# A hybrid decoder trunk on one core: SwiGLU's first products as paired 512-column streams, with modulation steps shifted later

## The chip, the cores and the metric

The kernel runs on one core of a Trainium2 chip. The metric is the device time of one execution in microseconds (us). Engine names follow the profile: PE is TensorE's matrix product, PEld its weight loads, DVE is VectorE, ACT is ScalarE, SP the queue that issues most transfers.

## The reference

Two layers, batch 1, 256 positions, width 1024, all in float32. Each layer is three residual blocks. Each block starts with an RMS norm and a modulation whose shift, scale and gate are parts of `silu(c) @ ada_w[l] + ada_b[l]` (a vector of 9 x 1024).

```python
h = _modulate(_rmsnorm(x, ffn1_norm[l]), sh1, sc1)
x = x + 0.5 * gt1 * _swiglu(h, ffn1_w_in[l], ffn1_w_out[l])   # (silu(a) * b) @ w_out, [a|b] = h @ w_in, 2816 wide
h = _modulate(_rmsnorm(x, mix_norm[l]), sh2, sc2)
...                                   # attention, conv and gated linear attention from one projection
x = x + gt2 * mixed
h = _modulate(_rmsnorm(x, ffn2_norm[l]), sh3, sc3)
x = x + 0.5 * gt3 * _swiglu(h, ffn2_w_in[l], ffn2_w_out[l])
```

## The kernel before

**Float32 as two parts.** Every weight and every operand is split into a high part and a low part of a type that PE multiplies in one pass. A product is high x high + weight high x operand low + weight low x operand high. `mm3` (L347 to L349) issues these as three matmuls of 256 columns, `mm2` (L353, L354) as one of 512 columns, whose moving operand is [high | low] side by side, and one of 256 columns. With `mm2` the two halves of a 512-column result still have to be added.

**A piece.** `split` loads 1 MB of a weight matrix (`raw`, 5 buffers, shared with the modulation's matrices), ACT copies it to the high part `wh` (L327, two tiles of 128x1024), DVE subtracts to get the low part `wl` (L328). `wh` and `wl` have 6 tiles each: three pieces. At the end of each `split` a planner (`PLAN`: steps m, lo, hi for each phase) issues steps of the modulation's product: each takes 1 MB of `ada_w` and one DVE instruction over 128x2048 (L232; the first of a group is L230). A group's sum goes through PE (L251, L263) two and three pieces later. `AT_END` issues further steps on PE near a phase's end.

**An FFN phase**, `ffn(l, i)`, four of them. The operand `hT` holds high and low for each of 8 k blocks, in rows of 258. Its first matrix has 22 pieces (11 for a, 11 for b). The first two are an `opening` that starts before the norm is known; the others go through `product`: 8 k x 2 halves x `mm3` = 48 matmuls into one PSUM bank (`wide`, tag "mm", four banks; a second set of four banks has the tag "tp"). ACT then reads a's bank (Silu, L369), DVE multiplies by b's bank (L592), and `split_out` (L642 on ACT, L643 on DVE) makes the two parts of the result. The second matrix has 12 pieces in four groups and uses `mm2`, with two banks for each group; DVE adds the results to the residual stream `xT` (L516). Phase (0, 0) differs: `open_first` does the first three products before it, so it counts 30 pieces and not 34.

**A mix phase** uses `product` for six matrices and `proj_n` (L670 to L672) for the others. The low-rank gate's product at L738 uses the [high | low] rows of `hT` as one 512-column operand.

The engines run their queues in the order in which the framework's planner wrote them; each queue is strictly in order.

Of the kernel before, what the change touches and what calls it, by code (L numbers as in the profile page):

```python
# [8 lines left out]
F32 = mybir.dt.float32  # L9
# [8 lines left out]
P = 128  # L18
# [33 lines left out]
EARLY = {(0, 1): (6,), (0, 2): (4,), (1, 0): (6,), (1, 1): (6,), (1, 2): (4,)}  # L52
LATE = 1
PART = 1024
FIRST, SECOND, AHEAD = 0, 2, 0
# [4 lines left out]
def trunk_kernel(ctx: ExitStack, tc: tile.TileContext, x, c, positions, ada_w, ada_b, ffn1_norm, ffn1_w_in,  # L60
# [24 lines left out]
    def bank(tag="tp"):  # L85
        return psum.tile([P, 512], F32, tag=tag, name=nm(tag), bufs=4)

    def wide():
        return bank("mm")

    def halves(t):
        return t.rearrange("p (a b) -> p a b", a=2)
# [212 lines left out]
    def split(src, shape, fine=False, held=None):  # L305
# [33 lines left out]
        m, tensor, lo, hi = PLAN[state["phase"]]  # L339
        at = lambda x: m * min(max(x - lo, 0), hi - lo) // (hi - lo)  # L340
        for x in range(at(state["piece"] - 1), at(state["piece"])):
# [9 lines left out]
    def mm2(o, wh, wl, pair, first, last):  # L351

        PE.matmul(o, wh, pair, start=first, stop=False)  # L353
        PE.matmul(o[:, 0:T], wl, pair[:, 0:T], start=False, stop=last)  # L354

# [148 lines left out]
    def product(w):  # L504

        wh, wl = w
        o = halves(wide())
        for k in range(KD):
            for s in range(2):
                cs = P * s, P * s + P  # L510
                mm3(o[:, s, :], wh(k, *cs), wl(k, *cs), high(k), low(k), k + s == 0, k + s == KD)
        return o

    def residual(o, l, i, d):
# [4 lines left out]
    def emit(d):  # L519

        if d % 2 == 0 and d < 6:
            return
        ds = [d] if d >= 6 else [d - 1, d]
        n = P * len(ds)
        t = halves(wide())
        ob = unit([P, 2, T], F32, "ob")
        for h in range(2):
            for i, e in enumerate(ds):
                PE.transpose(t[:, h, P * i:P * i + P], xT[:, e, P * h:P * h + P], ident)
        ACT.copy(ob[:, :, 0:n], t[:, :, 0:n])  # L530
        nc.sync.dma_start(out[0].rearrange("(h p) n -> p h n", p=P)[:, :, P * ds[0]:P * ds[0] + n], ob[:, :, 0:n])


    def ffn(l, i, w_in, w_out, done, first=None):
# [19 lines left out]
        if first is None:  # L554
            piece(1)
            pps = [[wide(), wide()] for _ in range(2)]
            opening(l, i, ws, pps, {HOOKS[l, i][0]: mean_square, HOOKS[l, i][1]: spread})
        else:
            ws += first[:4]
        for ch in range(KF // 2):  # L560
# [4 lines left out]
            if first is not None and ch < 2:  # L565
                if ch == 0:
                    continue
                pb = product(piece(3))
                opened, bias = first[4:]
# [10 lines left out]
            elif ch == 0:  # L580
                (a, ba), (b, bb) = rms(pps[0]), rms(pps[1])
                piece(1, SECOND)
                modulated(l, i)
                for s in range(2):
                    act(a[:, s, :], a[:, s, :], AF.Silu, bias=ba[:, s, :])
                    DVE.scalar_tensor_tensor(a[:, s, :], b[:, s, :], bb[:, s, :], a[:, s, :], op0=ALU.add,
                                             op1=ALU.mult)
            else:
                pa, pb = (product(piece(2 * ch + n, AHEAD)) for n in range(2))
                a = unit([P, 2, T], F32, "ab")  # L590
                act(a, pa, AF.Silu)
                DVE.tensor_mul(a, a, pb)  # L592
            gated(a)
        wo = w_out[l].rearrange("(k p) n -> p k n", p=P)
        late = []
        for grp2 in range(4):
            pp = [wide(), wide()]
            for k0 in range(0, KF, 8):
# [5 lines left out]
                for k, j in order:  # L604
                    g = gT[k0 + k]
                    mm2(pp[j], wh(k, P * j, P * j + P), wl(k, P * j, P * j + P), g, k0 + k == 0, k0 + k == KF - 1)
                while late:
# [38 lines left out]
    def mix(l, done):  # L646
# [12 lines left out]
        def proj_n(c0, n):  # L659

            nk = 2048 // n
            pp = [wide(), wide()]
            for k0 in range(0, KD, nk):
# [18 lines left out]
        ws = [split(wi[:, :, c0:c0 + 256], [KD, 256], fine=True) for c0 in (1792, 1536)]  # L682
        pps = [[wide(), wide()] for _ in range(2)]
        opening(l, 1, ws, pps, hooks={HOOKS[l, 1][0]: mean_square, HOOKS[l, 1][1]: spread})
# [231 lines left out]
        wo = mix_w_out[l].rearrange("(k p) n -> p k n", p=P)  # L916
        acc = [wide() for _ in range(4)]
        tile_of = lambda d: acc[d // 2][:, T * (d % 2):T * (d % 2) + T]
# [72 lines left out]
    def open_first():  # L991


        wi = ffn1_w_in[0].rearrange("(k p) (ab f) -> p k ab f", p=P, ab=2)
        held, ws, outs = [[] for _ in range(3)], [], []

        def load(m):
            ws.append(split(wi[:, :, m % 2, T * (m // 2):T * (m // 2) + T], [KD, T], fine=True, held=held[m]))

        def products(m, k0, k1):  # L1000
            if k0 == 0:
                outs.append(halves(wide()))
            wh, wl = ws[m]
            for k in range(k0, k1):
                for s in range(2):
                    cs = P * s, P * s + P
                    mm3(outs[m][:, s, :], wh(k, *cs), wl(k, *cs), high(k), low(k), k + s == 0, k + s == KD)
# [11 lines left out]
        for j in range(2):  # L1019
            for d2 in range(2):  # L1020
                t = halves(wide())
                for i in range(2):
# [105 lines left out]
```

## Time and profile before

| what | value |
|---|---|
| time, median of 3 runs | 1075.56 us (1074.71 to 1075.88) |
| time of the profiled execution | 1075.7 us |
| its span, first to last instruction | 1073.9 us |
| PE busy | 1053.9 us, 98% of the span |
| DVE busy | 817.0 us, 76% |
| ACT busy | 564.8 us, 53% |
| granted TensorE clock, mean | 0.994 of full speed |

PE's durations overlap: a matmul of 256 columns has a row of about 0.28 us and the next starts 0.12 us after it. What a matmul costs the stream is therefore the distance between starts, or a count over a stretch, and not its row's duration.

### The profile page before, as it was taken

Reading aid. Unit: us, or ns where it says so; the run is one execution under the profiler, and the core shown is the slowest. Engines: PE = TensorE matmul, PEld = TensorE weight load, DVE = VectorE, ACT = ScalarE, POOL = GpSimd, SP = SyncE. Lnnn points to the kernel's source line nnn. Section 1 sums busy time; section 2 is a strip of 40 time slices with the busy share of each in tenths; the row PEclk is TensorE's granted clock in tenths of the full one; section 3 lists DMA queues with packets and bytes.
Section 4 is the critical chain, followed back from the end, with each engine's and each line's share of the span. In section 5 each row is a group of like instructions: output and inputs, shape, how many; then the busy total and the mean of one; then the engine's idle time right before and its main releaser. Section 6 shows DMA issues by size and latency. Waiting matters only on the chain.

```text
span 1073.9 us, 19335 instructions
## 1 busy us (share of the span) xinstructions
PE 1053.9 (98%) x7899; PEld 970.3 (90%) x7899; DVE 817.0 (76%) x1310; ACT 564.8 (53%) x944; POOL 6.5 (1%) x30
## 2 busy tenths in 40 slices
PE   5999999999999999999999999999999999999998
PEld 4799998888888999998889999988878899999987
DVE  3598887979986898888569877766899688755552
ACT  4464454457665854444456444455757485444441
POOL 1000000000000000000000000000000000000000
PEclk8999999999999999999999999999999999999999
DMA  9989999995417389999667898876443446764540
GB/s 305 363 290 356 320 318 311 318 299 163 147 51 234 121 272 372 323 322 325 210 215 246 303 308 283 284 230 229 146 139 109 158 143 208 263 211 160 165 128 20
DMA packets 177593, 251.47 MB, mean 234 GB/s; under 512 B 7372, under 2 KB 156512, under 8 KB 170336
## 3 DMA queue, kind: packets, MB, share of 16 engines
q1 hardware_dynamic: 177272, 250.14, 69.4%
q8 instruction: 62, 1.02, 0.4%
q14 instruction: 27, 0.22, 0.1%
q10 hardware_dynamic: 232, 0.09, 0.0%
HBM read 249.16 MB, written 1.05 MB: 233 GB/s over the span
## 4 chain that ended last, share of the span: by engine, by line
PE 96%; DVE 1%; DMA 1%; ACT 1%; issue 0%; ACTq 0%; DVEq 0%
PE mm L347 18%; PE mm L349 17%; PE mm L348 17%; PE mm L353 15%; PE mm L354 8%; PE mm L671 3%; PE mm L670 2%; PE mm L672 2%; PE mm L923 2%; PE mm L924 1%; PE mm L922 1%; PE tp L223 1%; PE tp L828 1%; PE tp L801 1%; PE tp L251 1%; DMA held<-in_ffn_w_in_dram 1%
## 5 line engine op out<-in xcount | busy, mean ns | idle before, releaser
L327 ACT CAST wh<-raw 128x1024 fp32r<-128x1024 f32 (+1 forms) x352 | 338.8, 976 | 311.9 <-PE mm L348 126.4
L328 DVE TENSOR_TENSOR wl<-raw,wh 128x1024 fp32r<-128x1024 f32 (+1 forms) x352 | 392.2, 1129 | 140.2 <-ACT wh L327 130.4
L347 PE MATMUL mm<-hT,wh 128*128 128x256 f32 (+1 forms) x1568 | 445.6, 285 | 4.3 <-ACT hT L479 2.1
L349 PE MATMUL mm<-hT,wl 128*128 128x256 f32 (+1 forms) x1568 | 445.5, 285 | 0.0
L348 PE MATMUL mm<-hT,wh 128*128 128x256 f32 (+1 forms) x1568 | 444.6, 284 | 0.4 <-DVE hT L480 0.3
L347 PEld LDWEIGHTS mm<-hT,wh 128*128 128x128 f32 x1568 | 298.8, 191 | 11.1 <-issue 3.5
L348 PEld LDWEIGHTS mm<-hT,wh 128*128 128x128 f32 x1568 | 297.6, 190 | 1.7 <-DVE hT L480 1.0
L349 PEld LDWEIGHTS mm<-hT,wl 128*128 128x128 f32 x1568 | 297.5, 190 | 1.7 <-issue 1.6
L353 PE MATMUL mm<-g,wh 128*128 128x512 f32 x704 | 248.3, 397 | 0.0
L354 PE MATMUL mm<-g,wl 128*128 128x256 f32 x704 | 197.5, 280 | 0.0
L353 PEld LDWEIGHTS mm<-g,wh 128*128 128x128 f32 x704 | 132.0, 188 | 33.9 <-ACT wh L327 1.7
L232 DVE SCALAR_TENSOR_TENSOR adaacc<-adaraw,cact,adaacc 128x2048 f32<-128x2048 f32 (+1 forms) x59 | 123.5, 2093 | 14.4 <-DMA adaraw<-in_ada_w_dram 14.3
L354 PEld LDWEIGHTS mm<-g,wl 128*128 128x128 f32 x704 | 133.0, 189 | 0.0
L704 DVE SCALAR_TENSOR_TENSOR ab<-hpad,cw,ab 128x256 f32<-128x256 f32 x120 | 50.9, 476 | 0.0
L516 DVE SCALAR_TENSOR_TENSOR xT<-mm,gate,xT 128x256 f32<-128x256 f32 x80 | 34.5, 478 | 19.1 <-PE mm L354 18.8
L642 ACT CAST g<-ab 128x256 fp32r<-128x256 f32 x88 | 31.5, 403 | 32.3 <-DVE ab L592 32.0
L670 PE MATMUL mm<-wh,hT 128*128 128x512 f32 (+1 forms) x128 | 47.8, 373 | 0.0
L671 PE MATMUL mm<-wh,hT 128*128 128x512 f32 (+1 forms) x128 | 47.7, 373 | 0.0
L672 PE MATMUL mm<-wl,hT 128*128 128x512 f32 (+1 forms) x128 | 47.1, 368 | 0.0
L592 DVE TENSOR_TENSOR ab<-ab,mm 128x512 f32<-128x512 f32 x39 | 26.7, 685 | 17.0 <-PE mm L349 16.4
L923 PE MATMUL mm<-mix,wh 128*128 128x256 f32 x128 | 36.8, 291 | 0.2 <-DVE mix L643 0.2
L924 PE MATMUL mm<-mix,wl 128*128 128x256 f32 x128 | 36.0, 289 | 0.0
(208 smaller groups left out, 864.3 us busy)
## 6 DMA issues: line engine op xcount, KB each, us to landing
raw<-in_ffn_w_in_dram SPq DMA_DIRECT2D x85, 1024.0 KB
adaraw<-in_ada_w_dram SPq DMA_DIRECT2D x72, 1024.0 KB
raw<-in_ffn_w_out_dram SPq DMA_DIRECT2D x32, 1024.0 KB
raw<-in_mix_w_in_dram SPq DMA_DIRECT2D x24, 1024.0 KB
raw<-in_ffn_w_out_dram SPq DMA_DIRECT2D x16, 768.0 KB
raw<-in_mix_w_out_dram SPq DMA_DIRECT2D x8, 1024.0 KB
held<-in_ffn_w_in_dram SPq DMA_DIRECT2D x12, 256.0 KB
xn<-in_x_dram SPq DMA_DIRECT2D x4, 256.0 KB
```

The source lines that it names most:

```text
L232: DVE.scalar_tensor_tensor(part, w, cact[:, k, 0:1], part, op0=ALU.mult, op1=ALU.add)
L327: ACT.copy(hs[-1][:, b:c], raw_at(a + b, a + c))
L328: DVE.tensor_sub(ls[-1][:, b:c], raw_at(a + b, a + c), f32(hs[-1][:, b:c]))
L347: PE.matmul(o, wh, high, start=first, stop=False)
L348: PE.matmul(o, wh, low, start=False, stop=False)
L349: PE.matmul(o, wl, high, start=False, stop=last)
L353: PE.matmul(o, wh, pair, start=first, stop=False)
L354: PE.matmul(o[:, 0:T], wl, pair[:, 0:T], start=False, stop=last)
L670: PE.matmul(pp[t][:, 0:n], a, wh(k, 0, n), start=first, stop=False)
L671: PE.matmul(pp[t][:, 0:n], b, wh(k, 0, n), start=False, stop=False)
L672: PE.matmul(pp[t][:, 0:n], a, wl(k, 0, n), start=False, stop=last)
L923: PE.matmul(o, wh(i, *cs), mixT[k][:, T:2 * T], start=False, stop=False)
```

## The change

`product2` takes the place of `product` in the FFN phases (not in the openings, not in the mix phases): for each k and half one `mm2`, so 512 columns by the weight's high part and 256 by the low part, each half in a bank of its own. ACT then copies the low half out of PSUM and DVE adds the high half to it; Silu and the product with b now read SBUF. `wide` hands out two banks at a time, two buffers of them; `product` takes the first bank of such a pair. Transposes of the first stage and of the output move to the "tp" banks. In the planner a piece from the 21st on counts double.

```diff
+SECOND_FROM = 20
     def wide():
-        return bank("mm")
+        return psum.tile([P, 2, 512], F32, tag="mm", name=nm("mm"), bufs=2)
+
+    def pair():
+        t = wide()
+        return [t[:, 0, :], t[:, 1, :]]
...
         m, tensor, lo, hi = PLAN[state["phase"]]
-        at = lambda x: m * min(max(x - lo, 0), hi - lo) // (hi - lo)
+        weight = lambda x: min(max(x, lo), hi) + max(min(x, hi) - SECOND_FROM, 0)
+        at = lambda x: m * (weight(x) - weight(lo)) // (weight(hi) - weight(lo))
         for x in range(at(state["piece"] - 1), at(state["piece"])):
...
     def mm2(o, wh, wl, pair, first, last):
-        PE.matmul(o, wh, pair, start=first, stop=False)
-        PE.matmul(o[:, 0:T], wl, pair[:, 0:T], start=False, stop=last)
+        PE.matmul(halves(o), wh, pair, start=first, stop=False)
+        PE.matmul(o[:, 0:T], wl, pair[:, 0, :], start=False, stop=last)
...
     def product(w):
-        o = halves(wide())
+        o = halves(pair()[0])
...
+    def product2(w):
+        wh, wl = w
+        o = wide()
+        for k in range(KD):
+            for s in range(2):
+                cs = P * s, P * s + P
+                mm2(o[:, s, :], wh(k, *cs), wl(k, *cs), hT[:, k, :, 0:T], k == 0, k == KD - 1)
+        t = unit([P, 2, T], F32, "ab")
+        ACT.copy(t, o[:, :, T:2 * T])
+        DVE.tensor_add(t, t, o[:, :, 0:T])
+        return t
...
-                pb = product(piece(3))
+                pb = product2(piece(3))
...
-                pa, pb = (product(piece(2 * ch + n, AHEAD)) for n in range(2))
-                a = unit([P, 2, T], F32, "ab")
-                act(a, pa, AF.Silu)
-                DVE.tensor_mul(a, a, pb)
+                a, b = (product2(piece(2 * ch + n, AHEAD)) for n in range(2))
+                act(a, a, AF.Silu)
+                DVE.tensor_mul(a, a, b)
...
-            pp = [wide(), wide()]
+            pp = pair()
...
-        acc = [wide() for _ in range(4)]
+        acc = pair() + pair()
```

## Rows read from the trace of the kernel before

**Rows 1.** The page: the span, the engines' busy time, and the chain of work that ended last, by engine and by line.

```profile
span 1073.9 us, 19335 instructions
PE 1053.9 (98%) x7899; PEld 970.3 (90%) x7899; DVE 817.0 (76%) x1310; ACT 564.8 (53%) x944; POOL 6.5 (1%) x30
...
PE 96%; DVE 1%; DMA 1%; ACT 1%; issue 0%; ACTq 0%; DVEq 0%
```

**Rows 2.** Busy time by stretch: the steady parts of the four FFN phases' first matrices (80, 390, 580 and 890 us) and of their second matrices (170, 489, 684 and 1006 us). Columns: stretch, length, busy time and instruction count of each engine, granted clock, DMA share, GB/s.

```profile
80.00:160.00 80.00, 80.00 (x669) 79.03 (x669) 68.61 (x75) 36.91 (x54) 0.00 (x0) 1.00 0.96 331
...
170.00:220.00 50.00, 50.00 (x290) 42.83 (x289) 42.48 (x52) 24.02 (x35) 0.00 (x0) 1.00 0.93 315
390.00:480.00 90.00, 90.00 (x756) 89.46 (x756) 75.25 (x74) 41.86 (x57) 0.00 (x0) 1.00 0.98 342
489.00:550.00 61.00, 61.00 (x353) 51.47 (x352) 42.60 (x59) 28.46 (x43) 0.00 (x0) 1.00 0.75 245
...
580.00:680.00 100.00, 100.00 (x836) 99.03 (x835) 79.12 (x78) 46.86 (x63) 0.00 (x0) 1.00 0.90 306
684.00:745.00 61.00, 61.00 (x361) 52.37 (x360) 40.77 (x57) 28.31 (x42) 0.00 (x0) 1.00 0.72 231
890.00:1005.00 115.00, 115.00 (x954) 114.46 (x953) 73.28 (x88) 53.77 (x73) 0.00 (x0) 0.99 0.62 201
1006.00:1068.00 62.00, 62.00 (x359) 54.27 (x358) 27.79 (x36) 20.44 (x24) 0.00 (x0) 1.00 0.30 95
```

**Rows 3.** Stretches again, counting one line only: L349, the third matmul of `mm3`, so one for each triple (columns: PE, PEld, clock, DMA).

```profile
140.00:160.00 20.00, 15.81 (x56) 10.44 (x57) 1.00 0.89 304
390.00:420.00 30.00, 23.61 (x85) 15.76 (x84) 1.00 1.04 364
590.00:650.00 60.00, 47.31 (x168) 31.45 (x167) 1.00 0.91 311
910.00:960.00 50.00, 39.44 (x140) 26.18 (x139) 1.00 0.76 252
```

**Rows 4.** PE in order of time (start us, row's length us) in the second matrix of phase (1, 0): `mm2` pairs.

```profile
700.16 0.39 PE L353 MATMUL mm<-g,wh 128*128 128x512 f32 x1
700.39 0.28 PE L354 MATMUL mm<-g,wl 128*128 128x256 f32 x1
...
701.20 0.39 PE L353 MATMUL mm<-g,wh 128*128 128x512 f32 x1
```

**Rows 5.** The same in phase (0, 2).

```profile
500.09 0.40 PE L353 MATMUL mm<-g,wh 128*128 128x512 f32 x1
500.32 0.28 PE L354 MATMUL mm<-g,wl 128*128 128x256 f32 x1
500.44 0.40 PE L353 MATMUL mm<-g,wh 128*128 128x512 f32 x1
...
501.15 0.40 PE L353 MATMUL mm<-g,wh 128*128 128x512 f32 x1
```

**Rows 6.** PE in order of time in a mix phase: L738, whose moving operand is two runs of 256 out of `hT`'s rows of 258.

```profile
767.33 0.62 PE L738 MATMUL tp<-hT,wgs 128*96 128x512 f32 x2
767.79 0.39 PE L672 MATMUL mm<-wl,hT 128*128 128x512 f32 x1
```

**Rows 7.** Groups of instructions by line and shape (count, busy us, mean ns of one, idle time before them and what ended it).

```profile
L328 DVE TENSOR_TENSOR wl<-raw,wh 128x1024 fp32r<-128x1024 f32 x292 | 353.0, 1220 | 127.4 <-ACT wh L327 117.6 <-PE mm L354 7.7 <-PE tp L251 1.4
L232 DVE SCALAR_TENSOR_TENSOR adaacc<-adaraw,cact,adaacc 128x2048 f32<-128x2048 f32 x45 | 105.6, 2346 | 10.4 <-DMA adaraw<-in_ada_w_dram 10.3
...
L592 DVE TENSOR_TENSOR ab<-ab,mm 128x512 f32<-128x512 f32 x39 | 26.7, 685 | 17.0 <-PE mm L349 16.4
...
L327 ACT CAST wh<-raw 128x1024 fp32r<-128x1024 f32 x292 | 304.0, 1050 | 280.1 <-PE mm L348 119.1 <-PE mm L353 82.8 <-issue 64.9
...
L369 ACT ACTIVATE ab<-mm 128x512 f32<-128x512 f32 x39 | 23.1, 593 | 14.9 <-PE mm L349 14.9
```

**Rows 8.** DVE in order of time in phase (1, 0): from one reading of b's bank to the next (in brackets: idle time before, and what ended it).

```profile
636.81 0.69 DVE L592 TENSOR_TENSOR ab<-ab,mm 128x512 f32<-128x512 f32 x1
...
646.44 1.23 DVE L328 TENSOR_TENSOR wl<-raw,wh 128x1024 fp32r<-128x1024 f32 x1 [1.64 <-ACT wh L327]
649.23 2.35 DVE L232 SCALAR_TENSOR_TENSOR adaacc<-adaraw,cact,adaacc 128x2048 f32<-128x2048 f32 x1 [1.56 <-DMA adaraw<-in_ada_w_dram]
651.50 0.68 DVE L592 TENSOR_TENSOR ab<-ab,mm 128x512 f32<-128x512 f32 x1
```

**Rows 9.** Stretches of 10 us: the start of phase (0, 2)'s and of (1, 2)'s first matrix, and the stretch of the first matrix in which the transfers were fastest (columns as in rows 2).

```profile
370.00:380.00 10.00, 9.22 (x72) 8.78 (x73) 10.00 (x23) 6.20 (x13) 0.00 (x0) 1.00 0.27 89
...
420.00:430.00 10.00, 10.00 (x89) 9.46 (x87) 8.83 (x8) 3.94 (x6) 0.00 (x0) 1.00 1.04 380
880.00:890.00 10.00, 7.83 (x62) 7.42 (x61) 9.28 (x20) 8.03 (x19) 0.00 (x0) 0.98 0.92 315
890.00:900.00 10.00, 10.00 (x75) 10.00 (x74) 8.63 (x16) 4.91 (x9) 0.00 (x0) 0.85 0.17 46
```

More of the change, by code (lines that the diff above doesn't have):

```diff
@@ L524, in emit @@
         n = P * len(ds)
-        t = halves(wide())
+        t = halves(bank())
         ob = unit([P, 2, T], F32, "ob")
@@ L555, in ffn @@
             piece(1)
-            pps = [[wide(), wide()] for _ in range(2)]
+            pps = [pair() for _ in range(2)]
             opening(l, i, ws, pps, {HOOKS[l, i][0]: mean_square, HOOKS[l, i][1]: spread})
@@ L605, in ffn @@
                     g = gT[k0 + k]
-                    mm2(pp[j], wh(k, P * j, P * j + P), wl(k, P * j, P * j + P), g, k0 + k == 0, k0 + k == KF - 1)
+                    mm2(pp[j], wh(k, P * j, P * j + P), wl(k, P * j, P * j + P), halves(g), k0 + k == 0, k0 + k == KF - 1)
                 while late:
@@ L661, in proj_n @@
             nk = 2048 // n
-            pp = [wide(), wide()]
+            pp = pair()
             for k0 in range(0, KD, nk):
@@ L682, in mix @@
         ws = [split(wi[:, :, c0:c0 + 256], [KD, 256], fine=True) for c0 in (1792, 1536)]
-        pps = [[wide(), wide()] for _ in range(2)]
+        pps = [pair() for _ in range(2)]
         opening(l, 1, ws, pps, hooks={HOOKS[l, 1][0]: mean_square, HOOKS[l, 1][1]: spread})
@@ L995, in open_first @@
         held, ws, outs = [[] for _ in range(3)], [], []
+        banks = pair() + pair()
         def load(m):
@@ L1001, in products @@
             if k0 == 0:
-                outs.append(halves(wide()))
+                outs.append(halves(banks.pop(0)))
             wh, wl = ws[m]
@@ L1020, in open_first @@
             for d2 in range(2):
-                t = halves(wide())
+                t = halves(bank())
                 for i in range(2):
```

## The prediction, made before the changed kernel was run

> **What bounds the kernel now.** I read the page first: PE is busy 98% of the span and holds 96% of the chain that ended last [rows 1]. The stretches say the same of each FFN phase: PE is busy for the whole of every one, DVE for 45 to 86%, ACT for about half, the transfers run at 95 to 342 GB/s [rows 2]. So the end is set by the distance from one matmul's start to the next, and DVE, ACT and the transfers cost nothing as long as they stay ahead. The steady part of the first matrices counts 449 triples in 160 us; with one row's length of 0.28 us added for each of the four stretches (the first and last row are cut by the edges) that is 161.1 / 449 = 0.3588 us for a triple [rows 3]. A pair in the second matrices costs (701.20 - 700.16) / 3 = 0.3467 us in one phase [rows 4] and (501.15 - 500.09) / 3 = 0.3533 us in another [rows 5]. Both do the same arithmetic on 768 columns. These are two rhythms that the trace shows of the same instructions; I see no row that says which one a new stream will take.
>
> **The products.** `product2` replaces 79 of the 98 calls: 19 in phase (0, 0) (pieces 4 to 22) and 20 in each of the other three. Each has 16 triples that become pairs: 79 x 16 = 1264. At the quick rhythm a pair saves 0.3588 - 0.3467 = 0.0121 us, at the slow one 0.0055 us: 15.3 or 7.0 us in all. The two rows are equally near (same shapes, same kernel), so I take the middle, 0.0088 us: 11.1 us. One thing differs from the second matrix: the 512 columns come as two runs of 256 from rows of 258. L738 reads just these runs, and two of its matmuls take 767.79 - 767.33 = 0.46 us, 0.23 each [rows 6], as L353 does, 0.23 from its start to L354's [rows 4]. So I charge nothing for it. The Trainium skill (PSUM — Partial Sum Buffer, Specifications (TRN2)) says that any non-contiguous access pattern slows matmuls significantly; here the trace does not agree for this operand, 0.23 us with the gap and without; by that rule the saving could vanish altogether. The first product after each of three openings gains nothing, since DVE is what is late there: it is busy 10.00 of 10 us while PE has a gap of 0.8 us in the one, and PE gaps 2.2 us in the other [rows 9]. That gives back 3 x 16 x 0.0088 = 0.4 us. Sum so far: 10.7 us (6.6 to 15.3).
>
> **What it adds on ACT and DVE.** Each product gets one ACT copy of 128x512 out of PSUM and one DVE add of the same shape. The nearest rows are L369 with 0.593 us and L592 with 0.685 us [rows 7]; Silu and the multiplication stay, with SBUF instead of PSUM operands, which I cost as the same. That is 79 x 0.593 = 47 us on ACT and 79 x 0.685 = 54 us on DVE. It lies beside PE if they have room. Before, a product lasted 16 x 0.3588 = 5.74 us; after, 16 x 0.350 = 5.60. DVE's work for each product, from its share of the stretch [rows 2], plus the add, less the moved steps (below, 2.35 us each [rows 7]):
> (0, 0): 0.858 x 5.74 = 4.92 + 0.69 - 0.183 x 2.35 = 5.18 us, 92% of 5.60;
> (0, 2): 0.836 x 5.74 = 4.80 + 0.69 - 0.213 x 2.35 = 4.99, 89%;
> (1, 0): 0.791 x 5.74 = 4.54 + 0.69 - 0.168 x 2.35 = 4.84, 86%;
> (1, 2): 0.637 x 5.74 = 3.66 + 0.69 = 4.35, 78%.
> ACT comes to 0.461 x 5.74 + 0.59 = 3.24 us, 58%. Both stay below PE, and the splits run up to three pieces (17 us) ahead: most of ACT's idle time before a cast ends when PE frees a tile [rows 7]. So the bulk costs nothing; without that lead, (0, 0) would still hold.
>
> **The new wait.** Four banks become two buffers of two. Product n+2 can start only when the add of product n has read its buffer, so ACT's copy and DVE's add have 5.60 us from the end of n. Before, a bank had about three products. Behind the copy on ACT stand the next casts, behind the add on DVE the next subtractions and steps, and PE itself waits for the add. How late is DVE? The read of b's bank at 636.81 started as the product ended; two products later (11.48 us) the next ended at 648.3, and the read began at 651.50 [rows 8]: 3.2 us late, because a modulation step stood in front of it, which waited 1.56 us for its transfer and took 2.35. With that lateness the buffer is free after 3.2 + 0.69 = 3.9 us, 1.7 us in time. One more long instruction ahead (2.35 us) makes 6.25 us, and PE waits 0.65. The bounds are 0 (never more than the lateness shown) and 59 x 0.65 = 38 us (each product of the three busier phases). The shown lateness is inside the margin, so I take a value near the lower end: two or three such waits, 1.5 us.
>
> **The moved steps.** A piece from the 21st on counts double. By piece 20 phase (0, 0) has 11 steps issued instead of 14 (0.55 for each piece instead of 0.733), (0, 2) 9 instead of 12 (0.613, before 0.826), (1, 0) 7 instead of 9 (0.484, before 0.652); (1, 2) ends at piece 14 and does not move. Afterwards the rates are 1.10, 1.23 and 0.97. Each step moves its DVE instruction and its 1 MB transfer, on SP's queue past the weight pieces; the sums on PE stay as many and come due before the phase's end. In the second matrices a piece lasts on average 176 / 12 x 0.350 = 5.13 us. DVE there had 85% in (0, 0), 70% in (0, 2) and 67% in (1, 0) [rows 2]; the added 0.367, 0.40 and 0.316 steps for each piece bring 17, 18 and 14%: 102, 88 and 81%. Only (0, 0) is over, by 1 us in its last ten pieces, hidden by the three pieces of lead. The transfers are tighter. (0, 0) wants 9 MB of weights and 11 of steps, 21.0 million bytes in 144 pairs or 50.4 us, 416 GB/s; (0, 2) wants 7.5 + 10 MB in 42 us, 437. The first matrix showed 380 at best [rows 9], 342 in the mean of its fullest stretch [rows 2]: the transfers fall 5 to 11 us and 6 to 12 us behind. Five buffers of 1 MB (14 us at 380 GB/s) cover it, and they can fill beforehand, since the first part now asks only about 290 to 305 GB/s. Cost nothing; up to 10 us if that cover is used up.
>
> **The sum.** 1075.7 (the profiled execution, 0.1 above the median) - 10.7 + 1.5 = **1066.5 us**. Less than 0.2% (2.2 us) this kernel's runs can't tell from no change.
>
> **The rivals.**
> *The buffers are too few, slower.* DVE at 92 and 89% keeps a queue, and the add regularly stands behind a step and a pair of subtractions. Each such product costs PE 0.65 us. 17 of the 59 eat the gain, from 20 on it is a loss; at half of them it is 1075.7 - 10.7 + 19.5 = 1084.5 us. For it speaks the lateness of 3.2 us at a DVE load of only 79%; against it, that this lateness came from a late transfer, and the first part now has fewer of these. 0.13.
> *The second half is short of transfers, no change.* If weights and steps together leave only two buffers of lead, (0, 0) and (0, 2) wait some 5 and 6 us: 1075.7 - 10.7 + 11 = 1076 us. For it: DVE already waits 10.3 us for steps' transfers [rows 7]. Against: the lead of converted pieces behind the buffers. 0.08.
> *The pair is no cheaper than the triple in this place*, because the gap in the operand or the change of bank costs the 9 ns: 1075.7 + 1.5 = 1077 us. Against it: rows 4 and 6. The Trainium skill (TensorE: Matmul & The Clock Gate, Back-to-back issue gap) gives 262 cycles for 256 columns and 518 for 512; by it a pair saves 6 cycles, an estimate of 3.2 us in all, and the sum would be 1074.4; the trace's triple and pair differ by more, 5.5 to 12.1 ns. 0.05.
>
> **How the numbers follow.** The forecast has 0.74; its own range is 1060.5 (quick rhythm, no wait) to 1073 (slow rhythm, 4 us of waits). The range 1060 to 1076.5 takes in the second rival and leaves out the first, the third and a little below. Faster 0.74; same 0.12 (second and third rival); slower 0.14.
>
> **What would show it.** In the changed profile the triples of the first matrices become pairs at 0.347 or 0.353 us; ACT and DVE grow by about 47 and 54 us; PE's waits on DVE's add stay under 2 us together; the steps show less DVE and DMA load before the second matrices and more in them. The forecast fails if PE shows repeated waits at the first matmul of a product, or for `wh` and `wl` in the second matrices of (0, 0) and (0, 2). A gap of 2 us also costs afterwards: behind the one at 880 us the granted clock was 0.85, and 10 us held 75 matmuls instead of 86 [rows 2, 9].

## The result and the profile after

The change makes the kernel slower: 1087.25 us (median of 4, 1085.14 to 1088.66) beside 1075.23 us for the kernel before on the same chip (4 runs, 1074.71 to 1075.88). The ratio is 1.0110, with a 95% interval of 1.0092 to 1.0128. The forecast was 1066.5 us, in a range of 1060 to 1076.5. It is 21 us too low, and the sign is wrong.

The page of the changed kernel, the lines that answer to [rows 1, 7]: span, busy time, the chain by engine and the first matrices' 512-column products; then, from its groups by line, DVE's new adds and ACT's new copies. In the changed kernel L361 and L362 are `mm2`, L355 to L357 `mm3`.

```profile
span 1086.8 us, 16967 instructions
PE 1053.9 (97%) x6635; PEld 905.6 (83%) x6635; DVE 863.6 (79%) x1389; ACT 608.4 (56%) x1023; POOL 6.6 (1%) x30
...
PE 93%; DVE 2%; ACT 2%; DMA 1%; issue 0%; ACTq 0%
...
L361 PE MATMUL mm<-hT,wh 128*128 128x512 f32 x1264 | 448.7, 398 | 3.9 <-ACT ab L377 2.4
```

```profile
L532 DVE TENSOR_TENSOR ab<-ab,mm 128x512 f32<-128x512 f32 x79 | 53.7, 680 | 2.4 <-ACT ab L531 2.2
L531 ACT COPY ab<-mm 128x512 f32<-128x512 f32 x79 | 45.8, 579 | 2.2 <-PE mm L362 2.2
```

The 1264 triples are pairs, as meant. The copies and adds cost 45.8 us on ACT and 53.7 us on DVE. In all 1264 first matmuls of the pairs, PE waited 3.9 us. So the costly part is not where the new products run. But PE's share of the chain fell from 96% [rows 1] to 93%: for 3% more of the span than before, the end now hangs on other engines.

The stretches of the changed kernel: its first 60 us, then steady parts of the first three phases' first matrices (columns as in rows 2).

```profile
0.00:60.00 60.00, 42.48 (x413) 33.53 (x417) 27.02 (x63) 26.75 (x55) 4.57 (x26) 0.84 0.94 317
80.00:160.00 80.00, 80.00 (x457) 68.78 (x457) 73.87 (x93) 46.02 (x68) 0.00 (x0) 1.00 0.93 312
390.00:480.00 90.00, 90.00 (x517) 78.00 (x516) 84.59 (x95) 50.74 (x73) 0.00 (x0) 1.00 0.90 308
...
600.00:680.00 80.00, 80.00 (x456) 69.84 (x455) 70.36 (x74) 44.19 (x63) 0.00 (x0) 1.00 0.88 302
```

And the first 60 us of the kernel before:

```profile
0.00:60.00 60.00, 47.61 (x476) 40.15 (x477) 29.88 (x66) 30.81 (x60) 4.55 (x26) 0.91 0.93 318
```

In the steady parts PE is busy all the time, with DVE at 92, 94 and 88%. In the first 60 us PE is busy 5.1 us less, with 413 matmuls in place of 476, and its mean granted clock is 0.84 instead of 0.91.

PE's waits in the changed kernel (total us, times, longest us), without the first two rows of the list, which belong to the first 16 us and have their like in the kernel before:

```profile
PE mm L355 <- ACT hT L440: 3.1, 2, 1.5
PE tp L1089 <- DVE shift L1082: 2.9, 1, 2.9
PE mm L355 <- DVE ab L474: 2.5, 2, 2.0
PE mm L361 <- ACT ab L377: 2.4, 1, 2.4
```

No row of that list has PE waiting for L532, the add that frees a buffer in steady state. The sign that the prediction had named for its own failure, repeated waits at the first matmul of a product, did not show. What PE waits for is in the first stage (L440 makes the operand, L1082 copies the shift) and at the products that follow an opening (L474 reads the opening's bank, L377 is an activation on ACT).

The loss by stage, from the traces: each stage ends where the same instruction starts in every kernel (for the first stage the transposes that follow its products; then the first and last `g` matmul of each second matrix). Columns are microseconds more or less than the kernel before. "e2" to "e11" are experiments told below.

```
stage                         before   after     e2     e5     e6    e11
first stage                     58.8    +8.0   +6.3   +0.7   -0.5   +0.8
(0,0) rest of first matrix     105.7    -1.9    0.0   -0.9   -1.8   -1.9
(0,0) second matrix             64.4    -0.4    0.0   +0.4   +0.4   +0.4
mix 0 and (0,2) first          260.2    +3.3   +5.4   +7.8   +2.7   +4.4
(0,2) second matrix             64.6    +1.3    0.0   +0.1   +1.3   +1.4
(1,0) opening, first           130.5    +0.5   +0.7   -1.7   -3.4   +0.5
(1,0) second matrix             63.5    +1.5    0.0   +1.0   +1.5   +1.5
mix 1 and (1,2) first          258.1    -0.4   +2.8   -1.6   -3.1   +1.0
(1,2) second matrix             63.0     0.0    0.0    0.0    0.0    0.0
```

Eight of the twelve microseconds are lost before the first steady product; a last one lies behind the last row. The pairs do save time where nothing interrupts them (-1.9 us for 304 pairs in (0,0)). The two mix rows hide a loss behind a gain. Up to its last output matmul the first mix phase is 9.6 us longer and the second 4.1, and the first matrices behind them are 6.3 and 4.5 us shorter. In the first mix phase some 3 us of this is order alone, 26 more matmuls ahead of that point (948, before 922); in the second the count is the same. In e6 the two mix phases are 3.2 and 0.0 us longer.

### The profile page after: what moved, and what is told of

The parts are those of the page before. It is cut to its first block, busy times and chain, and to the rows that moved or that the text cites. A ratio compares the mean times of both kernels' runs of the same rounds, so it can differ in the third digit from the quotient of the medians.

```text
span 1086.8 us, 16967 instructions
## 1 busy us (share of the span) xinstructions
PE 1053.9 (97%) x6635; PEld 905.6 (83%) x6635; DVE 863.6 (79%) x1389; ACT 608.4 (56%) x1023; POOL 6.6 (1%) x30
## 4 chain that ended last, share of the span: by engine, by line
PE 93%; DVE 2%; ACT 2%; DMA 1%; issue 0%; ACTq 0%
PE mm L361 42%; PE mm L362 22%; PE mm L356 3%; PE mm L355 3%; PE mm L357 3%; PE mm L690 2%; PE mm L692 2%; PE mm L691 2%; PE mm L943 1%; PE mm L942 1%; PE mm L944 1%; PE tp L230 1%; ACT wh L334 1%; PE tp L821 1%; PE tp L848 1%; DVE wl L335 1%
## 5 line engine op out<-in xcount | busy, mean ns | idle before, releaser
L361 PE MATMUL mm<-hT,wh 128*128 128x512 f32 x1264 | 448.7, 398 | 3.9 <-ACT ab L377 2.4
L362 PE MATMUL mm<-hT,wl 128*128 128x256 f32 x1264 | 355.9, 282 | 0.0
L361 PEld LDWEIGHTS mm<-hT,wh 128*128 128x128 f32 x1264 | 239.6, 190 | 63.5 <-ACT hT L447 2.6
L361 PE MATMUL mm<-g,wh 128*128 128x512 f32 x704 | 249.1, 398 | 0.0
L362 PEld LDWEIGHTS mm<-hT,wl 128*128 128x128 f32 x1264 | 238.9, 189 | 0.5
L362 PE MATMUL mm<-g,wl 128*128 128x256 f32 x704 | 197.4, 280 | 0.0
L361 PEld LDWEIGHTS mm<-g,wh 128*128 128x128 f32 x704 | 132.1, 188 | 36.0 <-issue 2.5
L362 PEld LDWEIGHTS mm<-g,wl 128*128 128x128 f32 x704 | 133.0, 189 | 0.0
L355 PE MATMUL mm<-hT,wh 128*128 128x258 f32 (+1 forms) x304 | 88.5, 292 | 6.5 <-ACT hT L440 3.1
L356 PE MATMUL mm<-hT,wh 128*128 128x258 f32 (+1 forms) x304 | 88.6, 292 | 1.4 <-DVE hT L441 0.7
L357 PE MATMUL mm<-hT,wl 128*128 128x258 f32 (+1 forms) x304 | 87.0, 287 | 0.0
L355 PEld LDWEIGHTS mm<-hT,wh 128*128 128x128 f32 x304 | 58.5, 193 | 9.4 <-ACT hT L440 3.6
L356 PEld LDWEIGHTS mm<-hT,wh 128*128 128x128 f32 x304 | 58.5, 193 | 3.7 <-DVE hT L441 2.0
L357 PEld LDWEIGHTS mm<-hT,wl 128*128 128x128 f32 x304 | 58.7, 193 | 0.1
L532 DVE TENSOR_TENSOR ab<-ab,mm 128x512 f32<-128x512 f32 x79 | 53.7, 680 | 2.4 <-ACT ab L531 2.2
L690 PE MATMUL mm<-wh,hT 128*128 128x512 f32 (+1 forms) x128 | 47.5, 371 | 0.0
```

What stands on the lines that cost most here:

```text
L355: PE.matmul(o, wh, high, start=first, stop=False)
L356: PE.matmul(o, wh, low, start=False, stop=False)
L357: PE.matmul(o, wl, high, start=False, stop=last)
L361: PE.matmul(halves(o), wh, pair, start=first, stop=False)
L362: PE.matmul(o[:, 0:T], wl, pair[:, 0, :], start=False, stop=last)
L532: DVE.tensor_add(t, t, o[:, :, 0:T])
```

## The experiments

**The change taken apart: e1, e2, e3.** Theory A is the grouping of PSUM's banks in twos; theory B the planner. What the new products cost or gain with their copies and adds is the difference of e2 and e3.

e1, the kernel before with the planner's line alone:

```diff
-        at = lambda x: m * min(max(x - lo, 0), hi - lo) // (hi - lo)
+        weight = lambda x: min(max(x, lo), hi) + max(min(x, hi) - SECOND_FROM, 0)
+        at = lambda x: m * (weight(x) - weight(lo)) // (weight(hi) - weight(lo))
```

> The kernel before with the planner's double counting from the 21st piece as its only edit. Theory A (the banks: the changed kernel is already 8 us late after the first stage and loses 9 and 4 us in the two mix phases because its result banks come in two pairs): the planner is innocent, 1075 us, within 2 us of before, and each mix phase keeps its length (128 and 125 us). Theory B (the moved steps: they come due at the phases' ends and leave VectorE behind for the mix phase): the first mix phase is longer by about 5 to 9 us and the time is 1080 to 1084 us.

Measured: 1075.58 beside 1075.07 us, ratio 0.9998 (0.9988 to 1.0008). The moved steps cost nothing with the old products.

e2, the changed kernel with the old products and the old planner: only `wide` and `pair` as changed, and the transposes in the "tp" banks.

```diff
...
-                a, b = (product2(piece(2 * ch + n, AHEAD)) for n in range(2))
+                pa, pb = (product(piece(2 * ch + n, AHEAD)) for n in range(2))
...
```

> The changed kernel with the old products (three matmuls of 256 columns into one bank, no copy, no add) and the old planner: only the regrouping of the result banks into two pairs is left, with the transposes of the first stage in the other four banks. Theory A: the whole loss and none of the gain, 8 us in the first stage and 10 to 13 in the mix phases, 1093 to 1097 us. Theory B: only the first stage is late, 1083 us at most, and the mix phases keep 128 and 125 us.

Measured: 1091.94 beside 1075.07 us, ratio 1.0159 (1.0144 to 1.0174). The regrouping alone loses 17 us, more than the whole change; that is 1 us under theory A's range and 9 above theory B's. `product` uses one half of a two-bank tile here, so the grouping also leaves it two buffers where it had four. e2 has both effects in it, and no experiment parts them.

e3, the changed kernel with the old planner (`SECOND_FROM = 99`):

> The changed kernel with the old planner (new products and new banks stay). Theory A: within 3 us of the changed kernel, 1084 to 1090 us. Theory B: the mix phases go back to 128 and 125 us and the time to 1074 to 1080 us.

Measured: 1087.83 beside 1075.07 us, ratio 1.0115 (1.0091 to 1.0139). That is 4 us below e2, the new products' net gain on grouped banks; and it can't be told from the changed kernel, so B is out here as well.

**Is it the transposes' new place? e4.** The changed kernel with the input's transposes back in "mm" banks:

```diff
...
-                t = halves(bank())
+                t = halves(spare.pop(0))
```

> The changed kernel, with the four transposed tiles of the first stage back in the four result banks (as two pairs, handed back before the first products); nothing else is undone. Theory A for the first stage: the transposes had to share the other four banks with the modulation's sums, so the lateness of 8 us at 60 us goes and the time is 1079 us. If the lateness has another source (the two pairs held from the start, or a slower clock), it stays at 1085 us or more.

Measured: 1086.39 beside 1075.07 us, ratio 1.0106 (1.0089 to 1.0123); the first stage stays 7.9 us longer. Theory A's 1079 us for this edit missed: the move to "tp" is not the cause. (e4 puts the transposes into two-bank tiles; e11 below leaves them in "tp" and still has the first stage back.)

**The same products on single banks: e5, e6.** e5 is the kernel before with `product2` over two banks that are separate tiles, each half copied and added by itself; e6 has the planner's change besides.

```diff
+        o = [wide(), wide()]
...
+                mm2(o[s], wh(k, *cs), wl(k, *cs), hT[:, k, :, 0:T], k == 0, k == KD - 1)
+        t = unit([P, 2, T], F32, "ab")
+        for s in range(2):
+            ACT.copy(t[:, s, :], o[s][:, T:2 * T])
+            DVE.tensor_add(t[:, s, :], t[:, s, :], o[s][:, 0:T])
```

> The kernel before with the new products, but each half of a product in a bank of its own out of the four single ones (a copy of 128x256 and an add of 128x256 for each half), transposes and planner as before. Theory A2 (a tile of two banks is one thing to the framework: who reads one half waits for the matmuls into the other, and products in two halves of one tile can't be interleaved): the first stage is back at 59 us, the mix phases at 128 and 125 us, the first matrices 2 to 5 us shorter each, 1063 to 1068 us. Rival (four banks for two products in flight are the loss, however they are grouped): the first stage is back, but mix phases or first matrices stay 4 us or more longer, 1075 to 1083 us.

> The same as e5 and the planner's double counting from the 21st piece. From the planner-only run (no difference) I expect the time of e5 within 2 us. If the added copies and adds make VectorE short in the first matrices, this one is 2 to 5 us faster than e5.

Measured beside 1075.60 us: e5 1080.59, ratio 1.0041 (1.0026 to 1.0056); e6 1073.23, ratio 0.9981 (0.9970 to 0.9991). In e5 the rival's forecast came out: the first stage is back, mix 0 with the first matrix of (0,2) is 7.8 us longer, and the time lies in 1075 to 1083 us. But e6, on the same four banks, is 7.4 us faster still, where I had expected 5 at most; so four banks for two products are not the loss as such. Theory A2's 1063 to 1068 us was not reached by either. e6 differs from the changed kernel in the grouping (with it go the copies by halves, the transposes' place, which e4 and e11 cleared, and the two buffers of `product`), and it is 14 us faster. It and e12, which starts from it, are the only versions whose interval lies below the kernel before, if by no more than the 0.2% that these runs can tell. Its ten runs take 1071.51 to 1075.84 us, and the four longest are the four with a mean granted clock of 0.991; the others have 0.993 to 0.995. It also shows that the planner's change, worth nothing with triples, is worth 7 us here. Much of that can be the clock: its mean is 0.988 in e5's profiled run and 0.994 in e6's, and 0.6% of 1080 us is 6.5 us (an estimate, and an upper one, since PE also waits). What e6 still waits for most is the operand of the first product after two openings, (0,2) and (1,2): first its row of PE's waits, then the one in (0,2) in PE's order of time (in e6 L356 is `mm2`'s first matmul, L483 makes the operand's low part).

```profile
PE mm L356 <- DVE hT L483: 5.8, 2, 2.9
```

```profile
374.40 0.47 PE L356 MATMUL mm<-hT,wh 128*128 128x512 f32 x1 [2.91 <-DVE hT L483]
```

**The lateness of the residual alone: e7.** In a two-bank tile the residual's first read waits for the second half's last matmul. e7 is the kernel before with that lateness made by another means: the last piece no longer ordered by halves, so that both end together.

```diff
-                if grp2 == 3 and k0 + n == KF:
-                    order.sort(key=lambda t: t[1])
```

> The kernel before, with one edit: in the last piece of an FFN phase's second matrix the matmuls are not sorted by output half, so both halves end together and the first residual addition starts about 2 us later, as in the changed kernel. Theory A2: this lateness alone lengthens what follows an FFN phase (mix phases and openings) by 1 to 2 us in three places and the end by 1, 1078 to 1081 us. Rival (the opening covers it): 1075 to 1076 us.

Measured: 1075.02 beside 1075.60 us, ratio 0.9996 (0.9987 to 1.0006). The rival held: with single banks the late residual costs nothing, and theory A2 as I had put it for the openings is too simple.

**More room for the first products: e8.** The changed kernel with the second matrices' results in two single "tp" banks.

```diff
-            pp = pair()
+            pp = [bank(), bank()]
```

> The changed kernel, with the second matrices' results in two single banks of the other four instead of a two-bank tile; first stage, products and mix phases stay as changed. Theory A2: the first residual addition starts 2 us before the last matmul again, and the mix phases and openings after an FFN phase get 1 to 2 us shorter each: 1081 to 1085 us. Rival: no difference, 1086 to 1088 us.

Measured: 1090.49 beside 1075.60 us, ratio 1.0132 (1.0117 to 1.0148), slower than either forecast. PE now does wait for L532, 2.2 us in two waits, and the second mix phase with its FFN phase's first matrix is 5.6 us longer than in the changed kernel. A shortage of "tp" banks would fit, but PE's waits don't show one.

**The first stage: e9, e10, e11.** Its three products go through `banks`. Before, PE's queue held products of the second matrix while the first one's operand was still missing. In the changed kernel, matrices 0 and 1 are halves of one tile, and PE takes them strictly one after the other: 24 matmuls up to 26.7 us, a wait of 1.53 us for L440 that ends at 31.2, then 24 more. The kernel before has 42 without a wait at 28.3 to 33.9 us. e9 puts 0 and 1 into different tiles, with 2 beside 0. e10 also alternates the tiles of the mix output.

```diff
-        banks = pair() + pair()
+        ba, bb = pair(), pair()
+        banks = [ba[0], bb[0], ba[1]]
```

```diff
-        acc = pair() + pair()
+        ca, cb = pair(), pair()
+        acc = [ca[0], cb[0], ca[1], cb[1]]
```

> The changed kernel in which the three products of the first stage take halves of different two-bank tiles: matrix 0 the first half of tile A, matrix 1 the first half of tile B, matrix 2 the second half of A. Nothing else differs from the changed kernel (1086 to 1087 us). Theory 'a two-bank tile is one thing to the order of the queues': matrices 0 and 1 are free of each other again, as before the change, so PE's queue again holds products of the second matrix between those of the first, the first stage ends near 59 us and not 67, and the time is 1078 to 1080 us. Rival 'the late start comes from something else in the regrouping, such as fewer free banks or the copies' place': the first stage stays near 66 us and the time at 1086 to 1087 us.

> The kernel with the first stage interleaved, and beside it the four banks of the mix phase's last product taken in the order first of A, first of B, second of A, second of B, so that the residual's read of one bank and the matmuls into the next lie in different tiles. Theory 'one thing to the order of the queues': PE's short waits for the residual's reads at the ends of the two mix phases (0.4 to 0.9 us each in the changed kernel) go, and the time is 1 to 3 us under that of the kernel with the first stage alone, 1076 to 1078 us. Rival: the mix phases' loss is that of the openings that follow, and the time is the same as with the first stage alone within 1 us.

Measured beside 1075.41 us: e9 1089.26, ratio 1.0125 (1.0105 to 1.0145); e10 1088.73, ratio 1.0123 (1.0106 to 1.0140). Both expectations of theory A missed on the time, and e10 is as e9 within 1 us, as its rival had it. Half of e9's came true: PE's queue in e9 again has 42 matmuls at 28.6 to 34.3 us without a wait. What failed was the third product. It shares a tile with the first and waited 1.2 us for that one's read (L1079). DVE's queue in e9, in order of time:

```profile
50.77 0.69 DVE L1079 TENSOR_TENSOR ab<-mm,rsb 128x512 f32<-128x512 f32 x1 [4.72 <-PE mm L357]
51.38 2.49 DVE L335 TENSOR_TENSOR wl<-raw,wh 128x512 fp32r<-128x512 f32 x4
53.78 0.16 DVE L275 TENSOR_TENSOR mods<-tp,cols 128x8 f32<-128x8 f32 x1
...
53.98 0.29 DVE L1083 COPY shift<-mods 128x256 f32<-128x256 f32 x1
```

Four subtractions of the next piece (2.49 us) stand ahead of the 0.29 us copy for which PE waits. PE, in e9:

```profile
54.42 5.35 PE L1090 MATMUL tp<-held,shift 128*32 128x256 f32 x48 [3.47 <-DVE shift L1083]
```

So, as I read it, a lateness of some 2 us in one product turned an order round in a queue that is planned before the run, and that made a PE gap of 3.47 us; behind it the 48 matmuls took 5.35 us. e11 gives the third product a tile to itself as well.

```diff
-        banks = pair() + pair()
+        banks = [pair()[0], pair()[0], bank()]
```

> The changed kernel in which the three products of the first stage each have a tile to themselves: the first half of tile A, the first half of tile B, and a single bank of the transposes' set. With only matrices 0 and 1 apart, PE's products of the second matrix came early again, but the third product, in the tile of the first, waited for the first one's read (1.19 us), ended about 1.8 us later than before the change, and DVE did the next piece's subtractions ahead of the shift, so that PE waited 3.47 us for the shift and ran its next 48 matmuls in 5.35 us and not 2.80. Theory 'a tile of two banks orders everything in it': with the third one free too, the shift is again ahead of the subtractions, PE waits for it about 1 us, the first stage ends at 59 to 61 us, and the time is 1079 to 1083 us. Rival 'the order of DVE's queue at the start goes wrong for another reason (the shorter paired products behind it)': the first stage stays at 65 to 67 us and the time at 1086 to 1089 us.

Measured: 1083.64 beside 1075.50 us, ratio 1.0071 (1.0055 to 1.0086), 0.6 us above theory A's range and 2.4 below the rival's. The first stage ends at 59.6 us, in theory A's range. DVE and PE in e11, and the same instructions of the kernel before:

```profile
49.88 0.69 DVE L1078 TENSOR_TENSOR ab<-tp,rsb 128x512 f32<-128x512 f32 x1 [3.26 <-PE tp L357]
50.49 0.16 DVE L275 TENSOR_TENSOR mods<-tp,cols 128x8 f32<-128x8 f32 x1
50.68 0.29 DVE L1082 COPY shift<-mods 128x256 f32<-128x256 f32 x1
```

```profile
51.12 2.80 PE L1089 MATMUL tp<-held,shift 128*32 128x256 f32 x48 [1.02 <-DVE shift L1082]
```

```profile
50.23 2.80 PE L1068 MATMUL tp<-held,shift 128*32 128x256 f32 x48 [1.02 <-DVE shift L1061]
```

The order is back, and with it the wait of 1.02 us and the 2.80 us for the 48. The first stage's part of the loss is shown: 7.2 us of it (66.8 to 59.6) hang on which tiles the three products take; the one edit gives each a tile of its own, the third in the "tp" set.

**The openings: e12, e13, e14.** e12 asks whether e6's two waits of 2.9 us come from the paired product's need of two banks: there the first two products after an opening are triples in one bank again.

```diff
+                if ch == 1:
+                    pa, b = (product(piece(2 * ch + n, AHEAD)) for n in range(2))
...
```

> The kernel with single banks and the moved modulation (1073.2 us beside 1075.2) in which the first two products after each of the three openings are triples in one bank, as before the change. Theory 'the wait of 2.9 us behind the openings of (0, 2) and (1, 2) comes from the paired product's need of two banks there': the waits are 0.5 to 2.2 us as before the change, and the time falls by 2 to 3 us less the 96 pairs given up (0.6 us), to 1071 to 1072 us. Rival 'the order of DVE's queue there follows from something else, such as when the modulation's steps come due': the waits stay at 2.9 us and the time is 1073 to 1074.5 us.

Measured: 1073.83 beside 1075.50 us, ratio 0.9986 (0.9977 to 0.9995). The time is the rival's, as in e6. The waits went part of the way of the theory: two remain, now for ACT's part of the operand, of 2.2 and 2.1 us and not 2.9.

The changed kernel has a gap of 2.44 us after the opening of (1,0), which the kernel before does not have. PE there:

```profile
579.55 0.47 PE L361 MATMUL mm<-hT,wh 128*128 128x512 f32 x1 [2.44 <-ACT ab L377]
```

Stretches of the changed kernel around it:

```profile
573.00:577.00 4.00, 4.00 (x35) 3.91 (x33) 2.34 (x4) 2.84 (x5) 0.00 (x0) 1.00 0.19 33
577.00:579.00 2.00, 0.11 (x1) 0.00 (x0) 1.98 (x5) 2.00 (x8) 0.00 (x0) 1.00 0.87 348
579.00:583.00 4.00, 3.45 (x13) 3.00 (x14) 4.00 (x12) 2.22 (x8) 0.00 (x0) 0.66 0.13 55
583.00:587.00 4.00, 4.00 (x22) 3.46 (x22) 2.62 (x7) 2.60 (x6) 0.00 (x0) 0.92 0.00 0
```

Two dependencies of a two-bank tile could make it: the residual that starts late (e13 gives the last group of each second matrix two single banks), or the next product, which needs both reads of its tile (e14 gives the first matrix of each opening two single banks). Both start from e11.

```diff
-            pp = pair()
+            pp = pair() if grp2 < 3 else [bank(), bank()]
```

```diff
-            pps = [pair() for _ in range(2)]
+            pps = [[bank(), bank()], pair()]
```

> The changed kernel with the three separate tiles of the first stage (1083.6 us), in which the last of the four groups of each second matrix has two single banks of the transposes' set instead of a two-bank tile, so that the residual of its first half can be read while the second half is still being multiplied. Theory 'the late residual': the sums of squares come about 1.3 us earlier after the last matmul, as before the change, PE's gaps of 2.44 us in phase (1, 0) and 2.05 us in the second mix phase shrink to under 0.5, and the time falls by 5 to 7 us to 1077 to 1079 us. Rival 'the product after the opening waits for both reads of its tile': the gaps stay, at 1.5 us or more, and the time is 1082 to 1084 us.

> The changed kernel with the three separate tiles of the first stage (1083.6 us), in which the first of the two matrices of each opening has two single banks of the transposes' set and the second one a two-bank tile, so that the other two-bank tile is free for the product that follows. Theory 'the product after the opening waits for both reads of its tile': the gaps of 2.44 us in phase (1, 0) and 2.05 us in the second mix phase go or shrink under 0.5 us, and the time falls by 5 to 8 us to 1076 to 1079 us, if the transposes do with two banks. Rival 'the late residual': the gaps stay at 1.5 us or more, since the operand of that product comes late as well, and the time is 1082 to 1085 us.

Measured beside 1075.88 us: e13 1083.54, ratio 1.0066 (1.0045 to 1.0088); e14 1083.12, ratio 1.0066 (1.0050 to 1.0082). The gap in (1,0):

```profile
569.54 0.47 PE L361 MATMUL mm<-hT,wh 128*128 128x512 f32 x1 [0.74 <-DVE ab L474]
```

```profile
571.49 0.47 PE L361 MATMUL mm<-hT,wh 128*128 128x512 f32 x1 [0.65 <-DVE hT L488]
```

Either edit takes most of it away (0.74 in e13, 0.65 in e14, where under 0.5 had been expected), and the stage is 1.6 and 3.3 us shorter than in e11. In e13 a wait of 1.4 us for L532 comes up in the same stage, 13 us later. The times are those of the rivals, not of the theories: the second mix phase with its FFN phase's first matrix is 4.3 us (e13) and 2.9 us (e14) longer than in e11, and new waits stand there. Of e14 (the 3.5 us and the wait at L944 lie there, the one for L487 in the first mix phase):

```profile
PE mm L361 <- DVE hT L488: 5.3, 3, 3.5
...
PE mm L355 <- ACT hT L487: 2.9, 1, 2.9
...
PE mm L944 <- DVE wl L335: 2.0, 1, 2.0
```

So neither dependency is enough for the gap in (1,0) by itself: either edit shrinks it to 0.7 us. But the loss moves elsewhere. How the 10 us between e11 and e6 divide between the two dependencies, the two buffers that `product` has left in the mix phases, and an unlucky order of the queues stays open. That they hang on the grouping rests on e6 against the changed kernel.

## Why the prediction was wrong, point by point

**The step that failed** is "The new wait. Four banks become two buffers of two." I took it for a matter of `product2` alone and asked only whether the add frees a buffer in time; the term was 1.5 us. The diff also gives `pair()` to the first stage, the openings, the second matrices, the mix phases' products and the mix output, and for these the sum has no term at all. The grouping costs 17 us with the old products (e2) and 14 us with the new ones (the changed kernel against e6). 7.2 us of it are shown to come from products of the first stage that share a tile (e11); how the rest comes about is open.

**The bound of PE** held in the steady parts, with PE busy 80.00 of 80 and 90.00 of 90 us. It did not hold in the places between them, about which the profile's 98% says nothing: there a changed order of the queues made gaps that the kernel before did not have.

**The products.** The mechanism is right and the size too large. I counted 0.0088 us for each pair, the middle of two rhythms. From start to start, without interruptions, the triples of 256 columns of the kernel before have a mean of 0.3590 us (1292 of them) and the pairs of the changed one 0.3527 us (1226), so the slow rhythm for nearly all: 0.0063 x 1264 = 8.0 us and not 11.1. Even on single banks not all of that is left: e6 is 2.4 us faster than the kernel before. Among what it loses are its two waits of 2.9 us behind openings, where the kernel before has 0.8 and 2.1 [rows 9]. The 79 products are right, but 98 is the number of all matrices done in triples, those of the openings and the first stage among them; `product` is called 85 times, three times in each mix phase. The second matrices, which I left as they were, changed besides. That of (0,2) is 1.3 us longer because 12 more matmuls of the moved modulation lie in it (as in e1, where the first matrix is 1.5 us shorter for it). That of (1,0) is 1.5 us longer: its pairs have a mean of 0.3528 us instead of 0.3470, 1.0 us over 176 of them, and 4 more matmuls of the modulation lie in it. That rhythm was lost in e1, e3, e5 and e6 too, whatever part of the change they had, but not in e2.

**The gap in the operand** costs nothing that shows: 0.3527 us beside 0.3531 us in the second matrix of (0,2) of the kernel before, whose operand has no gap. The prediction had read the Trainium skill (PSUM — Partial Sum Buffer, Specifications (TRN2)) too widely: that row is about PSUM's cachelines, and this operand lies in SBUF, so no run here tests it. By the 262 and 518 cycles of the Trainium skill (TensorE: Matmul & The Clock Gate, Back-to-back issue gap) the pairs would save 3.2 us, an estimate; the trace gives 8.0. The sum by that estimate is 1074.1 us and not 1074.4, since the openings then give back 0.1 us and not 0.4.

**ACT and DVE** were right: +45.8 and +53.7 us of new work against 47 and 54, DVE at 92, 94 and 88% against 92, 89 and 86, and hidden in the steady parts.

**The rival "the buffers are too few"** would have been slower too, and its 1084.5 us lies nearer to the result than the forecast, but that is luck: in the changed kernel no wait for L532 is listed (e8 and e13 have 2.2 us each).

**The moved steps** cost nothing, as forecast (e1; e3 against the changed kernel). What I had not seen is that they can gain: 7 us on single banks (e5, e6), the clock's part in it included.

**What a gap costs.** The prediction had seen that a gap of 2 us is followed by a low granted clock, and did not ask what else could make such a gap. The two here, 2.86 us before L1089 and 2.44 us in (1,0), are followed by 48 matmuls in 5.35 us instead of 2.80, and by 4 us with a clock of 0.66, much as in [rows 9]. The prediction's "75 matmuls instead of 86" is 75 instead of 89 by [rows 9], and instead of 83 or 84 by the stretches of [rows 2].

## What to carry to other kernels

When two banks become one tile, list everything that is put into either bank, in every stage, and ask of each whether it may still start before its neighbour is read: what orders the queues sees the tile, not its halves. Short stages (a start, an opening, the end of a phase) belong in the sum by name, since a busy share over the span can't show that they are one late product away from a gap. If a wider copy and add is all that the grouping brings, keep single banks: e6 has the same products, with two copies and two adds for each in place of one, and is 14 us faster.

## What the runs showed of the hardware that I had not expected

A PE gap of 2.86 us before L1089 and the 3.47 us in e9 are each followed by the lower of TensorE's two levels (a granted clock of 0.50, 1.2 GHz): 48 matmuls took 5.35 us, beside 2.80 us behind a gap of 1.02 us, where the granted clock is 1.00. The changed kernel:

```profile
55.51 5.35 PE L1089 MATMUL tp<-held,shift 128*32 128x256 f32 x48 [2.86 <-DVE shift L1082]
```

```profile
55.50:60.90 5.40, 5.39 (x49) 2.56 (x49) 3.28 (x8) 3.45 (x9) 0.00 (x0) 0.50 0.70 233
```

The gap of 2.05 us in the second mix phase of the changed kernel is not: the granted clock is 1.00 in the 4 us behind it.

```profile
773.00:775.00 2.00, 0.15 (x2) 0.00 (x0) 1.98 (x5) 2.00 (x9) 0.00 (x0) 1.00 0.91 331
775.00:779.00 4.00, 3.80 (x24) 3.35 (x25) 4.00 (x11) 2.60 (x7) 0.00 (x0) 1.00 0.22 86
```

The length of the gap alone does not decide it. In e11 the same wait at the same place, again of 2.05 us, is followed by the lower level:

```profile
769.90:773.90 4.00, 4.00 (x17) 3.69 (x18) 4.00 (x11) 2.60 (x8) 0.00 (x0) 0.57 0.19 71
```

And of e6's two waits of 2.9 us the first is, the second is not:

```profile
374.40:378.40 4.00, 4.00 (x15) 3.38 (x16) 4.00 (x11) 2.11 (x5) 0.00 (x0) 0.66 0.00 0
889.00:893.00 4.00, 3.96 (x23) 3.50 (x24) 4.00 (x11) 2.44 (x6) 0.00 (x0) 1.00 0.21 84
```

What else decides is not shown.

The same instructions also keep one of two rhythms for tens of us: the pairs of (1,0) have a mean of 0.3470 us in the kernel before and 0.3530 us in e1, which has the same products and only other steps of the modulation beside them. In the second matrices of the kernel before, the changed one, e1 and e6, the rhythm changes only where other matmuls cut into the pairs. In (1,0) of the changed kernel the pairs take 0.3466 us up to the transposes of L270 at 700.8 us and 0.353 us behind them; in the kernel before nothing cuts in until 741.2 us, and they take 0.3466 us up to there. Not every cut changes the rhythm, and which one a stream starts in is not shown.
